# A weighted sum over eight experts: VectorE's work for 110 of 128 tokens as a hardware loop with semaphores of its own, and TensorE summing four terms of the last 18

## The chip, the cores and the metric

The kernel runs on one core of one Trainium2 chip. The metric is device time in microseconds, the median of several runs; a profile of one execution goes with it, and its span is measured from the first to the last instruction of the core.

## The reference

Each of 16 x 1024 tokens has eight expert outputs of 512 float32 numbers, and eight weights. The output of a token is the weighted sum of the eight.

```python
batch, seq, n_experts, expert_dim = 16, 1024, 8, 512
# expert_outputs: (16, 1024, 8, 512) float32; combine_weights: (16, 1024, 8) float32
weights = combine_weights[..., np.newaxis]
return np.sum(expert_outputs * weights, axis=2).astype(np.float32)
```

That is 268.4 MB read, 33.6 MB written and 0.5 MB of weights. With 128 partitions, every partition handles 128 tokens, and "a token" below means one row of 128 tokens, one on each partition: 16 KB of input and 2 KB of output per partition.

## The kernel before

A ring of ten token slots in SBUF takes the loads; `acc` has sixteen rows for sums. SyncE issues the loads as slots come free. For tokens 0 to 119 ScalarE makes the first product and VectorE adds seven terms with one operation each, the terms of two tokens taking turns. For the last eight tokens TensorE sums three terms, with diagonal matrices of the weights, and VectorE adds five. Stores of eight tokens are issued by ScalarE, the last ones by SyncE. A scheduler sets the semaphores; every instruction is written out, there is no loop on the chip.

```python
G = 8; SLOTS = 10; PE_TOKENS = 8; PE_EXPERTS = 3
x = expert_outputs.rearrange("b s e d -> (b s) e d").rearrange(
    "(n p g) e d -> n p g e d", p=P, g=G)
ring = one.tile([P, SLOTS, E, D], fp32, name="ring")
acc = one.tile([P, 2 * G, D], fp32, name="acc")
# ... loads: up to 4 tokens each, 2 from token 112 on, then pieces of the last two:
loads += [(T_P - 2, 1, 0, 4), (T_P - 2, 1, 4, 8)]
loads += [(T_P - 1, 1, 0, 3), (T_P - 1, 1, 3, 5), (T_P - 1, 1, 5, 7), (T_P - 1, 1, 7, 8)]

def first(i):
    s, a = i % SLOTS, i % (2 * G)
    if i < T_P - PE_TOKENS:
        pin(nc.scalar.mul(out=acc[:, a], in_=ring[:, s, 0], mul=w_t[:, i, 0:1]))
        return
    ps = ps_pool.tile([P, D], fp32, name="ps")
    for e in range(PE_EXPERTS):
        diag = diag_pool.tile([P, P], fp32, name="diag")
        pin(nc.scalar.mul(out=diag, in_=ident, mul=w_t[:, i, e : e + 1]))
        nc.tensor.matmul(ps, lhsT=diag, rhs=ring[:, s, e], start=e == 0, stop=e == PE_EXPERTS - 1)
    sums[i] = ps

def term(i, e):   # e >= 1, or >= 3 for the last eight tokens
    # ...
    pin(nc.vector.scalar_tensor_tensor(
        out=acc[:, a], in0=ring[:, s, e], scalar=w_t[:, i, e : e + 1],
        in1=before, op0=mult, op1=add))

for i in range(0, T_P, 2):
    load_until(i + SLOTS)
    for k in (i + 2, i + 3):
        if k < T_P: first(k)
    for e in range(E):
        for k in (i, i + 1): term(k, e)
    # ... store(end - G, G, nc.scalar) after every eighth token;
    # at the end 4 tokens (ScalarE's queue), then 2, 1 and 1 (SyncE's queue)
```

Of the kernel before, what the change touches and what calls it, by code (L numbers as in the profile page):

```python
# [1 line left out]

# [5 lines left out]


@with_exitstack  # L10
def kernel(
    ctx: ExitStack,
    tc: tile.TileContext,
    expert_outputs: bass.AP,
    combine_weights: bass.AP,
    out: bass.AP,
):

    nc = tc.nc
    fp32 = mybir.dt.float32
    mult, add = mybir.AluOpType.mult, mybir.AluOpType.add
    pin = tc.keep_in_program_order

    B, S, E, D = expert_outputs.shape
    T = B * S
    P = 128
    G = 8
    N = T // (P * G)
    T_P = N * G
    SLOTS = 10
    PE_TOKENS = 8
    PE_EXPERTS = 3

    x = expert_outputs.rearrange("b s e d -> (b s) e d").rearrange(
        "(n p g) e d -> n p g e d", p=P, g=G
    )
    w = combine_weights.rearrange("b s e -> (b s) e").rearrange(
        "(n p g) e -> p n (g e)", p=P, g=G
    )
    o = out.rearrange("b s d -> (b s) d").rearrange("(n p g) d -> n p g d", p=P, g=G)

    one = ctx.enter_context(tc.tile_pool(name="one", bufs=1))
    diag_pool = ctx.enter_context(tc.tile_pool(name="diag_pool", bufs=12))  # L50
    ps_pool = ctx.enter_context(
        tc.tile_pool(name="ps_pool", bufs=4, space=bass.MemoryType.PSUM)
    )

    ring = one.tile([P, SLOTS, E, D], fp32, name="ring")
    acc = one.tile([P, 2 * G, D], fp32, name="acc")
    w_t = one.tile([P, T_P, E], fp32, name="w_t")
    ident = one.tile([P, P], fp32, name="ident")


    loads = []
    BULK = 112
    t = 0
    while t < BULK:
        m = min(4, SLOTS - t % SLOTS, G - t % G)
        loads += [(t, m, 0, E)]
        t += m
    for t in range(BULK, T_P - 2, 2):
        loads += [(t, 2, 0, E)]
    loads += [(T_P - 2, 1, 0, 4), (T_P - 2, 1, 4, 8)]  # L70
    loads += [(T_P - 1, 1, 0, 3), (T_P - 1, 1, 3, 5), (T_P - 1, 1, 5, 7), (T_P - 1, 1, 7, 8)]
    loaded = 0

    def load_until(t):
        nonlocal loaded
        while loaded < len(loads) and loads[loaded][0] + loads[loaded][1] <= t:
            i, m, e0, e1 = loads[loaded]
            n, g, s = i // G, i % G, i % SLOTS
            if (e0, e1) == (0, E):
                dst, src = ring[:, s : s + m], x[n, :, g : g + m]  # L80
            else:
                dst, src = ring[:, s, e0:e1], x[n, :, g, e0:e1]
            pin(nc.sync.dma_start(out=dst, in_=src))  # L83
            loaded += 1

    sums = {}

    def first(i):

        s, a = i % SLOTS, i % (2 * G)  # L90
        if i < T_P - PE_TOKENS:
            pin(nc.scalar.mul(out=acc[:, a], in_=ring[:, s, 0], mul=w_t[:, i, 0:1]))  # L92
            return
        ps = ps_pool.tile([P, D], fp32, name="ps")
        for e in range(PE_EXPERTS):
            diag = diag_pool.tile([P, P], fp32, name="diag")
            pin(nc.scalar.mul(out=diag, in_=ident, mul=w_t[:, i, e : e + 1]))  # L97
            nc.tensor.matmul(  # L98
                ps, lhsT=diag, rhs=ring[:, s, e], start=e == 0, stop=e == PE_EXPERTS - 1
            )  # L100
        sums[i] = ps

    def term(i, e):
        s, a = i % SLOTS, i % (2 * G)
        if i < T_P - PE_TOKENS:
            before, e0 = acc[:, a], 1
        else:
            before, e0 = (sums[i] if e == PE_EXPERTS else acc[:, a]), PE_EXPERTS
        if e >= e0:
            pin(  # L110
                nc.vector.scalar_tensor_tensor(  # L111
                    out=acc[:, a],
                    in0=ring[:, s, e],
                    scalar=w_t[:, i, e : e + 1],
                    in1=before,
                    op0=mult,
                    op1=add,
                )
            )

    def store(i, m, queue):
        n, g, a = i // G, i % G, i % (2 * G)
        pin(queue.dma_start(out=o[n, :, g : g + m], in_=acc[:, a : a + m]))

    pin(nc.sync.dma_start(out=w_t.rearrange("p (n g) e -> p n (g e)", g=G), in_=w))  # L125
    make_identity(nc, ident)
    load_until(SLOTS - 2)
    for i in (0, 1):
        first(i)
    for i in range(0, T_P, 2):  # L130
        load_until(i + SLOTS)
        for k in (i + 2, i + 3):
            if k < T_P:
                first(k)
        for e in range(E):
            for k in (i, i + 1):
                term(k, e)
        end = i + 2
        if end <= T_P - G and end % G == 0:
            store(end - G, G, nc.scalar)  # L140
        elif end == T_P - 4:
            store(end - 4, 4, nc.scalar)
        elif end == T_P - 2:
            store(end - 2, 2, nc.sync)
        elif end == T_P:
            store(end - 2, 1, nc.sync)
            store(end - 1, 1, nc.sync)


# [1 line left out]
_INS = ['expert_outputs', 'combine_weights']  # L151
_OUTS = [((16, 1024, 512), 'float32')]


# [23 lines left out]
```

## Time and profile before

| | |
|---|---|
| time, median of 3 runs | 719.87 us (719.61 to 720.61) |
| span of the profiled execution | 718.5 us |
| VectorE busy | 585.6 us, 880 operations |
| ScalarE busy | 86.7 us, 145 operations |
| TensorE matmul busy | 28.0 us, 48 matmuls |
| loads (queue q1) | 270.01 MB, 87.3% of 16 engines' span |
| stores (queue q10) | 32.51 MB, 10.6% |
| HBM | 268.96 MB read, 33.55 MB written |

Busy shares are averages over the whole span; the slices of the span and the busy time by stage show which engine is full where. A row of the groups gives line, engine, operation and tiles, then the total busy time and the mean length of one in ns, then the idle time ahead of it with what ended it. A VectorE operation's length overlaps with the next one, so the distance between two is shorter than that length. A row of the DMA issues gives the number of transfers, the size of each, and the median time from issue to landing.

### The profile page before, as it was taken

Reading aid. Unit: us, or ns where it says so; the run is one execution under the profiler, and the core shown is the slowest. Engines: PE = TensorE matmul, PEld = TensorE weight load, DVE = VectorE, ACT = ScalarE, POOL = GpSimd, SP = SyncE. Lnnn points to the kernel's source line nnn. Section 1 sums busy time; section 2 is a strip of 40 time slices with the busy share of each in tenths; the row PEclk is TensorE's granted clock in tenths of the full one; section 3 lists DMA queues with packets and bytes.
Section 4 is the critical chain, followed back from the end, with each engine's and each line's share of the span. In section 5 each row is a group of like instructions: output and inputs, shape, how many; then the busy total and the mean of one; then the engine's idle time right before and its main releaser. Section 6 shows DMA issues by size and latency. Waiting matters only on the chain.

```text
span 718.5 us, 1363 instructions
## 1 busy us (share of the span) xinstructions
PE 28.0 (4%) x48; PEld 11.4 (2%) x48; DVE 585.6 (81%) x880; ACT 86.7 (12%) x145; POOL 0.7 (0%) x6
## 2 busy tenths in 40 slices
PE   0000000000000000000000000000000000000374
PEld 0000000000000000000000000000000000000131
DVE  0499888799697979897789787879897799997647
ACT  0210101111001110101110011111101101102210
POOL 0000000000000000000000000000000000000000
PEclk9999999999999999999999999999999999999967
DMA  9999999999999999999999999999999999999991
GB/s 372 441 427 420 423 438 420 455 406 462 423 425 440 449 405 436 447 431 440 429 415 453 431 425 440 422 430 447 424 441 435 434 416 436 436 431 434 427 405 73
DMA packets 11577, 302.59 MB, mean 421 GB/s; under 512 B 3120, under 2 KB 3120, under 8 KB 4016
## 3 DMA queue, kind: packets, MB, share of 16 engines
q1 hardware_dynamic: 9264, 270.01, 87.3%
q10 hardware_dynamic: 2304, 32.51, 10.6%
q14 instruction: 9, 0.07, 0.0%
HBM read 268.96 MB, written 33.55 MB: 421 GB/s over the span
## 4 chain that ended last, share of the span: by engine, by line
DMA 58%; DVE 36%; PE 2%; ACT 1%; issue 1%; DVEq 0%; SPq 0%; ACTq 0%
DMA ring<-in_expert_outputs_dram 58%; DVE acc L111 36%; PE ps L98 2%; ACT acc L92 1%; ACT L92 0%; DVEq L173 0%; SPq L125 0%; SPq L83 0%; ACTq L92 0%; DVEq L111 0%
## 5 line engine op out<-in xcount | busy, mean ns | idle before, releaser
L111 DVE SCALAR_TENSOR_TENSOR acc<-ring,w_t,acc 128x512 f32<-128x512 f32 x872 | 580.1, 746 | 111.6 <-ACT acc L92 111.6
L92 ACT ACTIVATE acc<-ring,w_t 128x512 f32<-128x512 f32 x120 | 77.6, 711 | 556.6 <-DMA ring<-in_expert_outputs_dram 556.5
L98 PE MATMUL ps<-ring,diag 128*128 128x512 f32 x48 | 28.0, 748 | 679.9 <-DMA ring<-in_expert_outputs_dram 675.7
L98 PEld LDWEIGHTS ps<-ring,diag 128*128 128x128 f32 x48 | 11.4, 245 | 695.6 <-issue 694.1
L111 DVE SCALAR_TENSOR_TENSOR acc<-ring,w_t,ps 128x512 f32<-128x512 f32 x8 | 5.9, 745 | 18.2 <-PE ps L98 18.2
L97 ACT ACTIVATE diag<-ident,w_t 128x128 f32<-128x128 f32 x24 | 7.9, 390 | 29.3 <-PE ps L98 21.8
L92 ACT ACT_TABLE_LOAD x1 | 1.3, 1283 | 25.9 <-DMA ring<-in_expert_outputs_dram 25.9
masks.py:199 POOL TENSOR_SCALAR_AFFINE_SELECT ident<-ident 128x128 f32<-128x128 f32 x1 | 0.3, 292 | 0.1
masks.py:197 POOL MEMSET ident<- 128x128 f32 x1 | 0.2, 205 | 0.3 <-POOLq L162 0.3
L162 POOL MEMSET const-bfloat16-1.0<- 128x1 bf16 x1 | 0.1, 102 | 0.0
L162 POOL MEMSET const-uint8-127<- 128x1 uint8 x1 | 0.1, 102 | 0.0
L162 POOL MEMSET const-float32-0.0<- 128x1 f32 x1 | 0.1, 98 | 0.2 <-issue 0.2
L162 POOL MEMSET const-float32-1.0<- 128x1 f32 x1 | 0.1, 98 | 0.0
## 6 DMA issues: line engine op xcount, KB each, us to landing
ring<-in_expert_outputs_dram SPq DMA_DIRECT2D x19, 4096.0 KB, 35.6
out_dram<-acc ACTq DMA_DIRECT2D x15, 2048.0 KB, 21.9
ring<-in_expert_outputs_dram SPq DMA_DIRECT2D x2, 1024.0 KB, 40.6
ring<-in_expert_outputs_dram SPq DMA_DIRECT2D x2, 512.0 KB, 25.9
out_dram<-acc ACTq DMA_DIRECT2D x1, 1024.0 KB, 7.7
ring<-in_expert_outputs_dram SPq DMA_DIRECT2D x1, 768.0 KB, 41.8
w_t<-in_combine_weights_dram SPq DMA_DIRECT2D x1, 512.0 KB, 4.1
out_dram<-acc SPq DMA_DIRECT2D x1, 512.0 KB, 2.7
```

What stands on the lines that cost most here:

```text
L92: pin(nc.scalar.mul(out=acc[:, a], in_=ring[:, s, 0], mul=w_t[:, i, 0:1]))
L97: pin(nc.scalar.mul(out=diag, in_=ident, mul=w_t[:, i, e : e + 1]))
L98: nc.tensor.matmul(ps, lhsT=diag, rhs=ring[:, s, e], start=e == 0, stop=e == PE_EXPERTS - 1)
L111: nc.vector.scalar_tensor_tensor(out=acc[:, a], in0=ring[:, s, e], scalar=w_t[:, i, e : e + 1], in1=before, op0=mult, op1=add,)
L162: nc = _bacc.Bacc("TRN2", target_bir_lowering=False, num_devices=1)
```

## The change

Tokens are taken in rounds of ten, so that a ring slot, a row of `acc` and a place in the loop are the same number. Eleven rounds (110 tokens) run on VectorE as a hardware loop, whose body is written once; the other engines' lists stay written out. ScalarE copies each round's weights to a fixed place, since the body's addresses don't change. VectorE makes the first product itself. Semaphores are set by hand: one for each of three chunks of a round (4, 4 and 2 tokens) for weights, load and store; VectorE takes the value off a semaphore after it has waited. For the last 18 tokens, ahead of which 32 diagonal matrices are made, TensorE sums four terms and VectorE adds four. The last two tokens are loaded in seven pieces whose order lets TensorE's four terms come first. It is for fewer instructions to be fetched and a shorter end.

The diff cut to its core:

```diff
-    G = 8
-    SLOTS = 10
-    PE_TOKENS = 8
-    PE_EXPERTS = 3
+    R = 10
+    FULL = T_P // R          # 12
+    ROUNDS = FULL - 1        # 11
+    LOOP = ROUNDS * R        # 110
+    TAIL = T_P - LOOP        # 18
+    CHUNKS = [(0, 4), (4, 4), (8, 2)]
+    PE_E = 4
+    DIAGS = 8 * PE_E
+    BANKS = 8
+    x_r = x[0:cut].rearrange("(n p r) e d -> n p r e d", p=P, r=R)
-    acc = one.tile([P, 2 * G, D], fp32, name="acc")
+    acc = one.tile([P, R, D], fp32, name="acc")
+    w_c = one.tile([P, R, E], fp32, name="w_c")
+    tail_loads = [(j, 2, 0, E) for j in range(0, R, 2)]
+    tail_loads += [(j, 1, 0, E) for j in range(R, TAIL - 2)]
+    a, b = TAIL - 2, TAIL - 1
+    tail_loads += [(a, 1, 0, 4), (b, 1, 0, 4), (a, 1, 4, 6), (b, 1, 4, 6)]
+    tail_loads += [(a, 1, 6, 8), (b, 1, 6, 7), (b, 1, 7, 8)]
+    tail_stores = [(0, 4), (4, 4), (8, 2)]      # ScalarE's queue
+    held_stores = [(R, 6), (a, 1), (b, 1)]      # SyncE's queue, after all loads
...
+    # SyncE
+                for n in range(ROUNDS):
+                    for c, (r, m) in enumerate(CHUNKS):
+                        if n:
+                            sync.wait_ge(done, (n - 1) * R + r + m)
+                        sync.dma_start(
+                            out=ring[:, r : r + m], in_=x_r[n, :, r : r + m]
+                        ).then_inc(loaded[c], 16)
...
+    # ScalarE
+                    for c, (r, m) in enumerate(CHUNKS):
+                        if n:
+                            scalar.wait_ge(done, (n - 1) * R + r + m)
+                            scalar.dma_start(
+                                out=o_r[n - 1, :, r : r + m], in_=acc[:, r : r + m]
+                            ).then_inc(stored[c], 16)
+                        if n < ROUNDS:
+                            scalar.copy(
+                                out=w_c[:, r : r + m], in_=w_t[:, n * R + r : n * R + r + m]
+                            ).then_inc(w_set[c], 1)
...
+    # VectorE
+                with nc.Fori(
+                    0, ROUNDS, engines=OrderedEngineSet([vector.engine]), head_slot={vector.engine: 0}
+                ):
+                    count["all"] = 0
+                    for c, (r, m) in enumerate(CHUNKS):
+                        take(w_set[c], 1)
+                        take(stored[c], 16)
+                        take(loaded[c], 16)
+                        for q in range(r, r + m, 2):
+                            for e in range(E):
+                                for k in (q, q + 1):
+                                    term(
+                                        k, e, 0, w_c[:, k, e : e + 1], acc[:, k] if e else None
+                                    )
+                    take(step, count["all"])
...
+                    if before is None:
+                        i = vector.tensor_scalar_mul(
+                            out=acc[:, r], in0=ring[:, r, e], scalar1=weight
+                        )
+                    else:
+                        i = vector.scalar_tensor_tensor(...)
+                    if e > first:
+                        i.wait_op(step, count[r], "sem-ge")
...
+    # TensorE, for each j of the last 18 tokens
+                    if j >= BANKS:
+                        tensor.wait_ge(done, LOOP + j - BANKS + 1)
+                    for e in range(PE_E):
+                        ...
+                        tensor.matmul(
+                            ps[:, j % BANKS],
+                            lhsT=diag[:, k % DIAGS],
+                            rhs=ring[:, j % R, e],
+                            start=e == 0,
+                            stop=e == PE_E - 1,
+                        ).then_inc(product, 1)
```

In the second weight load, SyncE brings the weights of the last eight tokens on their own. [...]

## The prediction, made before the changed kernel had run

> **What bounds the kernel now.** I read the page's table of 40 slices first, because a share over the whole span hides stages. Then the busy time by stage, the DMA issues, the timeline of VectorE, and the chain that ended last.
>
> ```profile
> DVE  0499888799697979897789787879897799997647
> DMA  9999999999999999999999999999999999999991
> GB/s 372 441 427 420 423 438 420 455 406 462 423 425 440 449 405 436 447 431 440 429 415 453 431 425 440 422 430 447 424 441 435 434 416 436 436 431 434 427 405 73
> DMA packets 11577, 302.59 MB, mean 421 GB/s; under 512 B 3120, under 2 KB 3120, under 8 KB 4016
> ```
>
> The DMA row is full from the first slice to the last but one; VectorE's row is not. So the transfers set the pace for some 700 us. In the busy time by stage the DMA share is 1.00 and the rate 430 to 436 GB/s in each 100 us stretch from 100 to 600, with VectorE busy 82 to 89 of each 100 us. The instruction row of the page then says what else uses these engines:
>
> ```profile
> q14 instruction: 9, 0.07, 0.0%
> L111 DVE SCALAR_TENSOR_TENSOR acc<-ring,w_t,acc 128x512 f32<-128x512 f32 x872 | 580.1, 746 | 111.6 <-ACT acc L92 111.6
> out_dram<-acc ACTq DMA_DIRECT2D x15, 2048.0 KB, 21.9
> out_dram<-acc SPq DMA_DIRECT2D x2, 256.0 KB, 2.1
> ```
>
> VectorE's 746 ns is the length of one operation, not the distance between two. The timeline gives the distance: a run with no gap,
>
> ```profile
> 619.82 20.62 DVE L111 SCALAR_TENSOR_TENSOR acc<-ring,w_t,acc 128x512 f32<-128x512 f32 x31
> ```
>
> so (20.62 - 0.746) / 30 = 0.6625 us from start to start. Each operation already waits on a semaphore of an operation two earlier here[...].
>
> The end is the other part. Busy time by stage, columns: window and its length, then PE, PEld, DVE, ACT, POOL busy, clock, DMA share, GB/s:
>
> ```profile
> 694.00:698.00 4.00, 3.73 (x5) 1.70 (x6) 2.14 (x4) 1.44 (x5) 0.00 (x0) 0.50 1.02 409
> 698.00:702.00 4.00, 4.00 (x8) 1.60 (x7) 0.75 (x1) 0.42 (x2) 0.00 (x0) 0.70 0.65 270
> 702.00:706.00 4.00, 4.00 (x11) 1.74 (x10) 3.26 (x5) 0.00 (x0) 0.00 (x0) 1.00 0.06 26
> 706.00:710.00 4.00, 1.85 (x5) 0.54 (x3) 4.00 (x7) 0.00 (x0) 0.00 (x0) 1.00 0.09 38
> ```
>
> A share of 0.06 from 702 to 706 is 1/16: one DMA engine still works while fifteen have finished. The packet records in the trace say the same: the last load completes at 705.95 us, on one engine some 6 us behind the rest. And after it comes serial work:
>
> ```profile
> 708.04 2.79 DVE acc L111 x5
> 710.83 0.51 issue
> 711.35 2.14 DVE acc L111 x4
> 713.48 0.51 issue
> 714.00 0.74 DVE acc L111
> ```
>
> Ten operations of the last two tokens run after their PE sums, then the last store lands at about 717.1, and 1.4 us of closing follow. So two things lie on the path: the byte flow up to 700, and 18 us in which almost nothing moves.
>
> [...]here a store's eight packets per engine pass one for one with load packets of 2.42 us, hence the 21.9 us of a store (8 x about 2.7). [...]nine 8 KB instruction packets inside the span, seven of them 87 to 106 us apart, and 880 / 7 = 126 of VectorE's operations to a packet.
>
> **The change part by part.**
>
> *Bytes.* The reference fixes 268.4 MB in, 33.6 MB out and 0.5 MB of weights. Ten tokens per partition are 10 x 128 x 18 KB = 23.59 MB, at 431 GB/s 54.7 us a round. Nothing changes here; loads are again 8 and 4 MB in the loop, with a distance of ten rows between partitions instead of eight.
>
> *VectorE in the loop.* ScalarE's 120 products of the first term (0.71 us each, hidden) move to VectorE for 110 tokens as a tensor-scalar. [...]A round is 70 x 0.6625 + 10 x 0.40 = 50.3 us, plus three waits for a chunk and one loop closing, for which I allow 1 to 2 us: 52, under the 54.7 of the bytes. [...]VectorE's work goes from 585.6 us to some 600 (110 x 5.03 = 553, and 72 x 0.6625 = 48), but it is packed into the loop, where its margin is thin.
>
> *Slack of the ring.* A four-token chunk takes 4 x 5.03 = 20 us and is refilled then. The DMA needs that place (4 + 2) x 5.47 = 33 us after the chunk landed. So 11 to 12 us of loads stay queued, and eleven rounds may run about 1 us each over the byte time before the DMA starves.
>
> *Stores and acc.* acc shrinks from sixteen to ten rows, so a chunk must be stored before VectorE writes its rows again one round later. Its store is issued about 21 us after its landing and takes some 22 to 30 us in turn with loads; it is needed 55 us after the landing. It fits, with a few us to spare.
>
> *Instruction fetch.* VectorE's 880 operations shrink to about 80 in the loop and 72 after it. The seven fetches become one or two. ScalarE, TensorE and SyncE have longer lists (72 weight tiles, 72 products), so I count five or six fetches in place of nine. Before, the spread between the first and the last engine of one load grows from 2.1 us to about 8 over nine fetches, and the spread first has to use up that engine's lead, so about 0.9 us each. Three or four fewer: the last load lands about 3.2 us earlier.
>
> *The end.* For the last two tokens TensorE has summed four terms while the rest is landing, and the last piece is one expert of one token. After it: one operation 0.75 us, a store of 256 KB 2.1 us. But a store of six tokens waits behind the loads in the same queue: 1.57 MB / 431 GB/s = 3.65 us. So the last store lands about 4.4 us after the last load instead of 717.1 - 705.95 = 11.15: 6.8 us saved.
>
> *Added.* A further barrier and branches ahead and behind, and a second weight load: about 1 us.
>
> Sum: 718.5 - 3.2 - 6.8 + 1 = 709.5 us of span. The time was 1.4 us over the profiled span: about **710.5 us**, 1.3% less.
>
> **The rivals.** (1) VectorE becomes the bound. For it: the margin is 2.7 us in 54.7, and the first term moved there. If the loop closing waits for a fetch of its own head each time (some us, and one more packet on the slow engine)[...], a round is 57 to 58 us and eleven rounds, less the 12 us of slack, add 15 to 25 us: 725 to 735. Against it: a body of about 95 instructions is below those 126 of one packet[...]. (2) Stores become the bound: three stores a round instead of 1.25, of eight packets per engine each, 24 store packets against 24 load packets. That is the one-for-one limit, so the store queue could grow and VectorE wait for it; the wait would fall inside the slack, and then cost a few us: 712 to 718. (3) The tail is hidden anyway: if the slow engine stays slow, only the 6.8 us remain, 713; if its lag vanishes, the last load lands near 700 and the span is 706.
>
> **Range and chances.** The flow of bytes, about 697 us, is common to all cases but the first rival, so the spread is small: the end and the fetches make 706 to 714, rival two 718. I take 705 to 716. Faster by over 2% needs under 705.5, which leaves 3 us after the flow and is nearly out of reach: 0.1. Slower by over 2% needs VectorE 25 us behind: 0.07.
>
> **What would show it.** Right: the DMA row full to the last slice but one; VectorE waiting for loads in every round; tensor-scalar operations about 0.4 us apart; fewer instruction packets than nine, and a spread of the last loads below 5 us; one operation and one store after the last load. Wrong: VectorE without gaps and a DMA share under 0.98 in the middle; waits for stores in the loop; eleven or more instruction packets; a steady rate other than 431 GB/s, from the new distance between partitions.

## The result and the profile after

The changed kernel takes 712.48 us (712.31 to 713.06 in four runs) against 720.24 us for the kernel before in the same comparison: a ratio of 0.9892, with a 95% interval of 0.9875 to 0.9909. The profiled span is 710.5 us, 8.0 us less than before.

The page of the changed kernel: the slices of the span, the row of instruction packets, the two kinds of VectorE operation in the loop, and the stores of four tokens.

```profile
DVE  0599899899899899899899899899899899954555
ACT  0000000000000000000000000000000140021200
...
DMA  9999999999999999999999999999999999999996
...
q14 instruction: 4, 0.03, 0.0%
...
L230 DVE SCALAR_TENSOR_TENSOR acc<-ring,w_c,acc 128x512 f32<-128x512 f32 x770 | 514.7, 745 | 0.0
...
L226 DVE TENSOR_SCALAR acc<-ring,w_c 128x512 f32<-128x512 f32 x110 | 48.3, 481 | 64.5 <-DVEq L219 64.5
...
out_dram<-acc ACTq DMA_DIRECT2D x24, 1024.0 KB, 26.8
```

The DMA row is full again, and now up to the last slice, which has a 6 where the kernel before has a 1. ScalarE, relieved of 120 products, is idle up to the weight matrices of the last tokens. VectorE is fuller in the loop and has one kind of gap only, ahead of a tensor-scalar, at line 219, which is the wait at the head of a chunk. Instruction packets fell from nine to four (a fifth, on a queue of its own, carries 0.02 MB). The timeline of VectorE inside the loop shows one such gap:

```profile
338.33 9.36 DVE L230 SCALAR_TENSOR_TENSOR acc<-ring,w_c,acc 128x512 f32<-128x512 f32 x14
350.54 0.88 DVE L226 TENSOR_SCALAR acc<-ring,w_c 128x512 f32<-128x512 f32 x2 [2.86 <-DVEq L219]
```

The end, as busy time by stage (the columns are those of the prediction's table):

```profile
694.00:698.00 4.00, 4.00 (x10) 1.71 (x9) 3.15 (x5) 0.00 (x0) 0.00 (x0) 1.00 1.01 398
698.00:702.00 4.00, 3.68 (x9) 1.33 (x7) 2.51 (x5) 0.00 (x0) 0.00 (x0) 1.00 0.57 234
702.00:706.00 4.00, 0.00 (x0) 0.00 (x0) 4.00 (x7) 0.00 (x0) 0.00 (x0) 0.83 0.47 200
```

The stretch with a share of 0.06, one engine of sixteen at work, is gone. From 702 to 706 the stores of the last tokens move while VectorE still has seven operations to do. The timeline says what those waited for (the page counts 144 matmuls for the 72 products of this kernel, two records for each, so the 48 counted for the kernel before are 24 products):

```profile
691.14 10.54 PE L208 MATMUL ps<-ring,diag 128*128 128x512 f32 x24 [1.24 <-issue]
...
699.49 0.74 DVE L230 SCALAR_TENSOR_TENSOR acc<-ring,w_t,ps 128x512 f32<-128x512 f32 x1
699.60 7.20 SPq L137 DMA_DIRECT2D out_dram<-acc  x3
...
701.72 0.75 DVE L230 SCALAR_TENSOR_TENSOR acc<-ring,w_t,ps 128x512 f32<-128x512 f32 x1 [1.49 <-PE ps L208]
702.38 4.06 DVE L230 SCALAR_TENSOR_TENSOR acc<-ring,w_t,acc 128x512 f32<-128x512 f32 x6
```

Twelve products for the last three tokens run without a gap from 691.14 to 701.68, and VectorE's first operation of the last token waits for them. Six more follow, until 706.44 (702.38 + 4.06), and the last of SyncE's three stores is issued then.

### The profile page after: what moved, and what is told of

The parts are those of the page before. It is cut to its first block, busy times and chain, and to the rows that moved or that the text cites. A ratio compares the mean times of both kernels' runs of the same rounds, so it can differ in the third digit from the quotient of the medians.

```text
span 710.5 us, 1687 instructions
## 1 busy us (share of the span) xinstructions
PE 69.5 (10%) x144; PEld 28.4 (4%) x144; DVE 604.5 (85%) x952; ACT 30.3 (4%) x106; POOL 0.7 (0%) x6
## 3 DMA queue, kind: packets, MB, share of 16 engines
q10 hardware_dynamic: 5184, 31.46, 10.5%
## 5 line engine op out<-in xcount | busy, mean ns | idle before, releaser
L230 DVE SCALAR_TENSOR_TENSOR acc<-ring,w_c,acc 128x512 f32<-128x512 f32 x770 | 514.7, 745 | 0.0
L208 PE MATMUL ps<-ring,diag 128*128 128x512 f32 x144 | 69.5, 637 | 632.2 <-DMA ring<-in_expert_outputs_dram 621.6
L226 DVE TENSOR_SCALAR acc<-ring,w_c 128x512 f32<-128x512 f32 x110 | 48.3, 481 | 64.5 <-DVEq L219 64.5
L208 PEld LDWEIGHTS ps<-ring,diag 128*128 128x128 f32 x144 | 28.4, 203 | 672.5 <-DMA ring<-in_expert_outputs_dram 624.1
L230 DVE SCALAR_TENSOR_TENSOR acc<-ring,w_t,ps 128x512 f32<-128x512 f32 x18 | 13.4, 746 | 37.4 <-PE ps L208 37.4
L230 DVE SCALAR_TENSOR_TENSOR acc<-ring,w_t,acc 128x512 f32<-128x512 f32 x54 | 36.5, 746 | 0.0
L182 ACT COPY w_c<-w_t 128x32 f32<-128x32 f32 (+1 forms) x33 | 6.8, 213 | 557.2 <-DVE acc L230 554.0
L161 ACT ACTIVATE diag<-ident,w_t 128x128 f32<-128x128 f32 x72 | 22.2, 388 | 84.6 <-PE ps L208 77.0
## 6 DMA issues: line engine op xcount, KB each, us to landing
out_dram<-acc ACTq DMA_DIRECT2D x24, 1024.0 KB, 26.8
out_dram<-acc ACTq DMA_DIRECT2D x12, 512.0 KB, 30.8
```

The lines of the kernel that those rows point to most:

```text
L161: i = scalar.mul(out=diag[:, k % DIAGS], in_=ident, mul=w_t[:, LOOP + j, e : e + 1],).then_inc(diag_set, 1)
L182: scalar.copy(out=w_c[:, r : r + m], in_=w_t[:, n * R + r : n * R + r + m]).then_inc(w_set[c], 1)
L208: tensor.matmul(ps[:, j % BANKS], lhsT=diag[:, k % DIAGS], rhs=ring[:, j % R, e], start=e == 0, stop=e == PE_E - 1,).then_inc(product, 1)
L226: i = vector.tensor_scalar_mul(out=acc[:, r], in0=ring[:, r, e], scalar1=weight)
L230: i = vector.scalar_tensor_tensor(out=acc[:, r], in0=ring[:, r, e], scalar=weight, in1=before, op0=mult, op1=add,)
```

## Where the 8.0 us came from

From the packet records of both traces, the moment when the last load has completed on all engines splits the span in three:

| | before, us | after, us | difference |
|---|---|---|---|
| last load complete | 705.95 | 700.63 | -5.32 |
| from there to the last store's landing | 11.16 | 7.52 | -3.64 |
| from there to the end of the span | 1.4 | 2.3 | +0.9 |

The load part contains a later start: the first load is issued at 2.24 us in place of 1.23, behind a further barrier and the second load of weights. The rest shows in the landings, of which the trace has sixteen for each load: the first of the last piece comes at 697.6 us in the kernel before and at 698.4 in the changed one, and the sixteenth 8.8 us after it in the one and 2.7 in the other. So the loads end earlier because the sixteen parts of a load land closer together.

## The experiments

The theories at the outset: (A) VectorE's instruction packets delay one DMA engine, and the loop takes them away; (B) the gain lies in the last tokens alone; (C) closing the loop costs something; (D) what costs is that VectorE waits for its own instructions. Times are medians; runs named side by side were on the same chip.

**VectorE's loop written out.** One part undone.

```diff
-                with nc.Fori(0, ROUNDS, engines=..., head_slot={vector.engine: 0}):
+                for _ in range(ROUNDS):
```

> VectorE's loop is written out, eleven bodies one behind the other; everything else is the changed kernel. Theory A (instruction packets of VectorE delay one DMA engine, about 0.97 us each): six or seven more instruction packets, the spread between the first and the last DMA engine of a load grows from 2.1 to some 6 to 8 us, the last load lands 4 to 6 us later, time 716 to 719 us. Theory B (the gain lies in the order of the last pieces and the four terms on TensorE alone): time within 1 us of the 712.5 of the changed kernel. Theory C (the loop's edges of 0.4 us cost something): 1 to 4 us less than 712.5.

Measured: 717.56 us, against 711.91 for a version with the loop (with another `head_slot`, see the next but one); ratio to the kernel before 0.9959, interval 0.9947 to 0.9971. The page's row of instruction packets and the busy time by stage near the end:

```profile
q14 instruction: 10, 0.08, 0.0%
```

```profile
696.00:700.00 4.00, 3.81 (x9) 1.82 (x10) 1.21 (x3) 0.00 (x0) 0.00 (x0) 1.00 0.68 263
700.00:704.00 4.00, 4.00 (x11) 1.72 (x10) 4.00 (x7) 0.00 (x0) 0.00 (x0) 1.00 0.06 26
```

The 1/16 is back: one engine works alone from 700 to 704. The last load completes at 705.52 us, 4.9 later than with the loop. The packet records show how the lag is built: the spread between the first and the last engine of a round's first load is 1.67 us up to the packet at 137 us, and then 2.31, 3.21, 4.15, 5.15 and 5.91 after the packets at 137, 213, 289, 364 and 440 us, and 7.11 after the one at 523; the next, at 600 us, adds 0.95 more, by the two-token load after it. A packet is busy for 0.31 us, but these seven widened the spread by some 0.9 us each on the mean: (7.11 + 0.95 - 1.67) / 7 = 0.91. The packet at 543 us, which the version with the loop has too (at 539 us), adds nothing to the spread. In the changed kernel the spread of a round's first load stays at 2.07 from 100 to 600 us. Theory A holds, and the loop is worth 5.1 us against the 712.48 of the changed kernel and 5.7 against the version beside it; B and C fall as to the loop. D falls too: in the eleven bodies VectorE's operations stand 0.66 or 0.40 us apart throughout, but for the heads of chunks, where it waits for loads. What is left against the kernel before, about 3 us, is the rest of the change; no run undoes that part alone.

**900 memsets more on GpSimd.** The same dose for an engine that nothing waits for.

```diff
+                for i in range(900):
+                    gpsimd.memset(spare[:, i : i + 1], 0.0)
```

> The changed kernel with 900 one-column memsets more on GpSimd, which nothing waits for: about seven more instruction packets, but for an engine off the path. Theory A1 (any instruction packet delays the DMA engine that brings it): a spread of 6 to 8 us and 716 to 719 us, as with VectorE's loop written out. Theory A2 (each engine's instructions come by another DMA engine, and the one for GpSimd has more lead): less, 713 to 716 us. Rival (what costs is that VectorE itself waits for its instructions): 712.5 us, no change.

Measured: 714.55 us, 2.6 more than the 711.91 beside it. The page's row:

```profile
q14 instruction: 11, 0.09, 0.0%
```

Seven packets more, all in the first 40 us. The spread of a round's first load is 5.08 us from 75 us on and stays there to 600. So GpSimd's instructions cost time though nothing waits for GpSimd and VectorE's waits at the heads of chunks are as long as before (65.0 us in all, 64.5 in the changed kernel), which speaks against D once more. The size agrees with A2 and not with A1. That the packets come by another DMA engine than VectorE's can be read from the trace. One packet of VectorE's comes at 652 us in the changed kernel and at 653 here (it is VectorE's, since it comes at 684.5 with `head_slot` 224). In the changed kernel it widens the spread of a two-token load from 1.76 to 2.62 us. Here the spread is 4.24 ahead of it and after it, and only the second-latest engine comes closer to the latest, from 2.27 to 1.42 us. So the latest one, which GpSimd's packets delay, is not VectorE's. Why seven packets cost 3 us of spread here and VectorE's cost more isn't settled: that an engine has some lead to use up first was only a guess, in A2 as in the prediction.

**`head_slot` 224 in place of 0.** The first rival of the prediction held that closing the loop might fetch its head again. Here only this parameter of the loop differs.

```diff
-  head_slot={vector.engine: 0}
+  head_slot={vector.engine: 224}
```

> [...]Theory R ([...]the loop closes without a fetch): one instruction packet more at most, time 712 to 714 us. Theory F (each closing of the loop fetches the first block again): ten or more instruction packets more, a wait of some us at each closing, spread of the loads 8 us and more, time 718 us or above.

Measured: 711.91 us, four instruction packets as in the changed kernel, spread 2.28 us. One packet comes at 684.5 us in place of 652, and none comes with a closing of the loop. Theory R holds in that: the loop closes without a fetch, here as with `head_slot` 0.

**The first term as a two-tensor operation, and twice.** How far is VectorE from being the bound?

```diff
-  k, e, 0, w_c[:, k, e : e + 1], acc[:, k] if e else None
+  k, e, 0, w_c[:, k, e : e + 1], acc[:, k] if e else zero
```

> The changed kernel with the first term in the loop as a two-tensor operation on a tile of zeros[...] (0.66 us in place of 0.40): a round of VectorE takes 53.1 us in place of 50.5. Theory (the bytes set the pace, 54.5 us a round): VectorE's waits for loads shrink from 38.7 to some 13 us, time 712 to 713.5 us. Rival (VectorE is already at the bound, or the later release of slots starves the loads): 29 us more over eleven rounds, at least 5 us more to be seen.

Measured: 712.49 us, no change. VectorE's waits for chunks shrink to 35.1 us, of which 24.6 are the first, so 10.5 are left of 38.7. Its busy time by stage:

```profile
200.00:300.00 100.00, 0.00 (x0) 0.00 (x0) 97.41 (x148) 1.28 (x6) 0.00 (x0) 1.00 1.00 433
```

With the first term made twice in the loop, the second over the first:

```diff
+                                for k in (q, q + 1) if e == 0 else ():
+                                    term(k, e, -1, w_c[:, k, e : e + 1], zero)
```

> The same with the first term made twice in the loop, the second over the first: 90 two-tensor operations, 60 us a round of VectorE against 54.5 of the bytes. Theory: now VectorE sets the pace; 5.5 us over eleven rounds is 61, of which the ring's slack takes some 5 to 12: time 760 to 770 us, VectorE without gaps in the loop, DMA share about 0.91 in the middle. Rival (the ring takes it up, or the DMA's pace is not what the loads wait for): under 740 us.

Measured: 758.32 us, 45.8 more than with the first term made once.

```profile
200.00:300.00 100.00, 0.00 (x0) 0.00 (x0) 100.00 (x152) 1.06 (x5) 0.00 (x0) 1.00 0.96 401
```

A stretch of VectorE's timeline, with the first operation of a round at 443.62:

```profile
434.34 9.36 DVE L232 SCALAR_TENSOR_TENSOR acc<-ring,w_c,acc 128x512 f32<-128x512 f32 x14
443.62 2.73 DVE L232 SCALAR_TENSOR_TENSOR acc<-ring,w_c,zero 128x512 f32<-128x512 f32 x4
```

VectorE has no gap any more, and the DMA engines deliver less: 389 to 401 GB/s in each 100 us from 100 to 600, where the run with one first term had 430 to 438. That is the 0.91 expected, though the share of busy time reads 0.94 to 0.96. The time is a little below the stated range. Rounds follow each other every 59.62 us, not 60, so 5.15 above the 54.47 of the bytes and 56.7 in eleven rounds. 45.8 of them reached the time: some 11 were taken up, as expected (5 to 12). The round that begins at 443.62 does so 0.66 us after the operation ahead of it, the distance of any two, so closing the loop costs nothing that can be seen.

**First halves of the third and fourth last tokens first.**

```diff
-    tail_loads += [(j, 1, 0, E) for j in range(R, TAIL - 2)]
+    tail_loads += [(j, 1, 0, E) for j in range(R, TAIL - 4)]
+    tail_loads += [(TAIL - 4, 1, 0, 4), (TAIL - 3, 1, 0, 4), (TAIL - 4, 1, 4, 8), (TAIL - 3, 1, 4, 8)]
```

> The changed kernel with the third and fourth last tokens loaded in halves too, both first halves ahead of both second halves. Theory (TensorE is late for the last two tokens, since its four products of the token before them start only when that token has landed whole): its last product ends about 1.9 us earlier, the last store lands 1.4 us earlier, time about 711 us. Rival (VectorE's eight operations for the last two tokens set the end, or the store of six tokens in the queue of the loads does): 712 to 713 us, no change.

Measured: 711.77 us, no difference from the 711.91 beside it. The timeline of TensorE:

```profile
681.80 12.23 PE L209 MATMUL ps<-ring,diag 128*128 128x512 f32 x24 [2.43 <-issue]
694.23 7.11 PE L209 MATMUL ps<-ring,diag 128*128 128x512 f32 x16 [0.19 <-issue]
```

The products of five tokens now run nearly without a gap from 681.80 to 701.34 and still end where they did (701.68). In the changed kernel a token takes 10.54 / 3 = 3.5 us; here the first three take 12.23 / 3 = 4.1, and the granted clock is 0.78 to 0.79 from 680 to 688, where the changed kernel had 1.00. The earlier start was spent on slower products. So this run doesn't decide whether the wait for TensorE sets the end; the next one does.

**TensorE's sum added last, for four tokens.** VectorE starts with its own terms and adds TensorE's sum at the end; in `order`, E stands for that addition.

```diff
+                    i = vector.tensor_tensor(out=acc[:, r], in0=acc[:, r], in1=ps[:, j % BANKS], op=add)
...
+                    late = q >= TAIL - 4
+                    if late:
+                        order[-1:] = [(E, q), (E - 1, q + 1), (E, q + 1)]
...
-                            acc[:, r] if e > PE_E else ps[:, j % BANKS],
+                            acc[:, r] if e > PE_E else None if late else ps[:, j % BANKS],
```

> The changed kernel, but for the last four tokens VectorE starts its own four terms as they land (a tensor-scalar first) and adds TensorE's sum at the end, with one operation more for each token. Theory (what follows the last load is VectorE's wait for TensorE's late products, and the queue of operations behind it): VectorE ends at about 702.5 in place of 705.8 us, one product-and-add and one add after the last load, time 709 to 710 us. Rival (VectorE's number of operations sets the end): four more operations, no gain or 1 to 3 us more.

Measured: 710.39 us, 2.1 less than the 712.49 beside it (the version with the first term as a two-tensor operation, as fast as the changed kernel), with four operations more. The timeline of VectorE at the end:

```profile
698.49 0.49 DVE L232 TENSOR_SCALAR acc<-ring,w_t 128x512 f32<-128x512 f32 x1 [0.80 <-DMA ring<-in_expert_outputs_dram]
698.89 3.40 DVE L236 SCALAR_TENSOR_TENSOR acc<-ring,w_t,acc 128x512 f32<-128x512 f32 x5
702.32 0.69 DVE L224 TENSOR_TENSOR acc<-acc,ps 128x512 f32<-128x512 f32 x1
702.92 0.74 DVE L236 SCALAR_TENSOR_TENSOR acc<-ring,w_t,acc 128x512 f32<-128x512 f32 x1
703.70 0.69 DVE L224 TENSOR_TENSOR acc<-acc,ps 128x512 f32<-128x512 f32 x1
```

VectorE ends at 704.39 (703.70 + 0.69), 2.05 us earlier than in the changed kernel, where it ended at 706.44; the 705.8 of the expectation was about the start of its last operation (705.7). It did not end at 702.5: it stood 0.80 us at a piece of the last token, which landed at 698.46 us. The rival falls, and the wait for TensorE was on the path.

**The order of the last ten operations.** The version that follows from it: both early terms of the last token but one (`a`) before the wait for the last token's piece (`b`).

```diff
+                    if q == TAIL - 2:
+                        order = [(4, a), (5, a), (4, b), (5, b), (6, a), (7, a), (6, b), (E, a), (7, b), (E, b)]
```

> As the version that adds TensorE's sum last (710.4 us), but VectorE takes both early terms of the last token but one before it waits for the last token's piece, which one DMA engine brings some 1.5 us late. Theory (VectorE stood 0.8 us at that piece with work at hand): one operation fewer after it, 0.5 to 0.8 us less, about 709.7 us, and 2.5 to 3 us less than the changed kernel. Rival (the chain of terms of one token, each waiting for the one before it, takes the gain back): 710 to 711 us.

The changed kernel ran beside it once more:

> The changed kernel once more, beside the next one on the same chip: 712 to 713 us, 0.987 to 0.991 of the kernel before.

Measured: 709.67 us for the new order and 712.63 for the changed kernel, on the same chip: 0.9853 (0.9837 to 0.9870) and 0.9895 (0.9879 to 0.9912) of the kernel before. It is faster than the changed kernel by 3.0 us. What the order alone adds to the sum added last isn't shown: that version had 0.9860 (0.9843 to 0.9876) of the kernel before on another chip, and the two intervals overlap.

## Why the prediction came out right, point by point

The time of 712.48 lies in the range, 2.0 us above the 710.5 of the text. The text's own sum gives 709.5 + 1.4 = 710.9, and the 1.4 compared a median with the span of another execution: the profiled one took 720.52 us for its span of 718.5, so 2.0 more. The span of 710.5 is 1.0 above the 709.5 forecast. That it is so close is in part luck: two terms were wrong in opposite directions, by 2 to 3 us each.

- *Bytes set the pace.* Right. The steady rate was 429 to 436 GB/s in each 100 us from 100 to 600, so ten rows between partitions in place of eight changed nothing. The DMA share was 0.99 to 1.01 in the same stretches; that no kernel could move more was not shown.
- *VectorE in the loop.* Right. Two tensor-scalars stand 0.40 us apart in the records (0.88 for two less the 0.48 of one). The 0.40 of the prediction was an assumption of mine, which no run had shown by then. Rounds follow each other every 54.5 us, the bytes' pace, and VectorE waits 2.86 and 1.10 us in each, so its work is 50.5 us a round against 50.3 and an allowance of 1 to 2, which was not needed: neither the closing of the loop nor the waits for weights and stores took time that can be seen.
- *Slack of the ring.* Right: with the first term made twice, some 11 of 56.7 us were taken up, where 11 to 12 was said.
- *Stores.* Right, with one length just outside: 26.8 us for four tokens and 30.8 for two, where 22 to 30 was said. A four-token store landed some 7 us before VectorE took its rows again (397.6 and 405.0, for instance). Of the three waits at a chunk's head, the trace shows time only in the third, the one for the load. The second rival falls. Its one-for-one shows in the packet records of the kernel before: while the 128 packets of a store of eight tokens went, 112 to 130 load packets began.
- *Instruction fetch.* The mechanism was right and the size was not. I counted the packets of all engines alike and took three or four fewer for 3.2 us. Writing the loop out showed what VectorE's own packets are worth: six more in all, and 4.9 us on the last load. The term of the sum was too small by about 2 us, since five packets went and not three or four, and the engine that lagged was VectorE's.
- *The end.* This step failed: "After it: one operation 0.75 us, a store of 256 KB 2.1 us." It assumed that TensorE had finished four terms of the last two tokens while the rest landed. TensorE needed 3.5 us a token and had three tokens to do from 691.14 on, so it ended 1.0 us after the last load, with seven of VectorE's operations behind it. The part saved 3.6 us, not 6.8, and adding TensorE's sum last took 2.1 more. The queued store of six tokens, which I thought would delay the last one, did not: it landed at 704.3 us, before VectorE was done (706.4).
- *Added.* 1.0 us at the start and 0.9 at the end, where I had 1 in all.

So: loads 5.3 us earlier in spite of a start 1.0 later, instead of 3.2 with it left out; the end 3.6 shorter instead of 6.8; and a closing part 0.9 longer.

## What to carry to other kernels

Where transfers fill the DMA engines, as here, look for a stretch at the end in which the share is 1/16 (0.06), and count instruction packets before blaming the loads: six more of them moved the last load from 700.63 to 705.52 us. A loop that shortened the longest list of instructions paid 5.1 us though its engine wasn't the bound. It could fill that engine nearly to the full, 97 to 99 of each 100 us with the first term as a two-tensor operation, without loss (712.49 us), as long as the engine still waited for loads; with the first term made twice and no wait left, the time rose by 45.8 us. Before handing the last tokens' terms to another engine, multiply its time for one token by the number that land close together, 3.5 us by three here; the sum added at the end of a chain forgave a late partner, the one added at its start did not, and the difference was 2.1 us.

## What was not expected of the hardware

An instruction packet of 8 KB is busy for 0.31 us in the records, yet VectorE's widened the spread of a load by about 0.9 us each, and they add up: with the loop written out, one DMA engine was at work alone from 700 to 704 us, a share of 0.06, and the last load was complete at 705.52. For this kernel, which is bound by its transfers, the loop is worth the measured 5.1 to 5.7 us. TensorE's products for three tokens took 12.23 us where the granted clock was 0.78 to 0.79 for about the first half, and 10.54 where it was 1.00 throughout.
